# Spreading a gated recurrence over the chunks of a weight stream, on one Trainium2 core

## The chip, the cores and the metric

One core of one Trainium2 chip runs the whole program. The metric is the device time of one execution in microseconds (us). Before the change it is 1965.23 us, the median of 3 runs (1964.89 to 1965.62). The core has a matrix engine (TensorE, PE in the profile; PEld is its weight load), VectorE (DVE), ScalarE (ACT), GpSimd (POOL) and SyncE (SP, which here starts the transfers of weights). Each engine runs its own instructions strictly in their order and waits for the others by semaphores. PSUM is the memory into which PE accumulates; SBUF holds everything else.

## What is computed

One layer of a decoder for a prompt of 256 tokens and 8 samples of 8 tokens, 320 columns T in all, that share every weight. Cut to what matters here:

```python
h = rmsnorm(x) * (1 + sc1) + sh1                 # sc, sh, g: silu(c) @ w_ada
q, k, v, og, u, ga, gb, alr = split(h @ w_in)
loga = log_sigmoid(alr @ w_a2 + b_a) / 16
o, s_new = gla(q, k, v, loga, s0)                # per head: S = decay * S + k'v, o = q S
y_a = rmsnorm(o) * silu(og)
y_b = (windowed_mean(u) - u) @ w_pool * pool_scale
merged = sigmoid(ga) * y_a + sigmoid(gb) * y_b
x = x + g1 * (merged @ w_o)
x = x + g2 * swiglu(rmsnorm(x) * (1 + sc2) + sh2)   # w_gu, w_down
```

There are 4 heads; the kernel calls what belongs to one head a group (0 to 3): its 256 columns of q, k and u, and its 512 of v, og, ga and gb.

## The kernel before

Weights come as chunks of 512 KB (`raw`, 3 buffers, SP's queue). ACT rounds each to `whi` (L159, a CAST of 128x512, two to a chunk), DVE takes the rest to `wlo` (L160), and PE forms every product as three matmuls (`mm3`, L198 to L200: whi with the high part of the activations, whi with the low part, wlo with the high part), each 128 rows by 320 columns. One whi and wlo feed 12 such matmuls. `proj` makes one unit, 256 output columns: 16 row blocks, 96 matmuls, into a PSUM tile `ps`. The main PSUM pool (`pmain`) has two tiles: a unit can't begin until the unit two before it has been evacuated. A second pool of four (`pmisc`, tiles `pm`) serves everything small.

The program has a head (conditioning, h, and all projections of group 0), then the mix stage, then w_o, w_gu and w_down. The mix stage projects groups 1 to 3, unit by unit (q, k, v twice, u, og twice, ga twice, gb twice; gb of groups 1 and 3 was made in the head, `EARLY_GB`), and beside this runs the recurrence of the group before. Its steps stand in a list, `queue`, and `pump(n)` takes n of them, all at once, after each unit: `RATE` is 10, so that a lump of ten steps stands between two units. `ada_step` puts blocks of 24 more matmuls (L250, a product with w_ada; the profile shows each as two) between the chunks, in step with the stream.

The steps that matter below: `s_gk` makes the log decay from gk (on ACT: Abs L774, Exp L776, Ln L778, each with a table load of its own, ACT_TABLE_LOAD, and then two casts, L782; DVE's part of the split is L783). `s_exp(0)` and `s_exp(1)` sum it up by matmuls (L795 and L796) and take exponentials on ACT (L800 to L805). `s_prod` multiplies these with q and k (DVE, L811 to L831). `s_vstack` casts v in eight pieces (ACT, L841). `s_norm` is the normalisation of o (a matmul L1000, Sqrt L1002 on ACT, reciprocal L1003 and four products L1005 on DVE). `merge_step` multiplies with the gates (L1098) and adds (L1099). `s_y` of the pooling is the product with w_pool (tiles `psy`), evacuated by L1090.

`evac` brings a unit out of PSUM: q and k on ACT (L385), into the one buffer `g.q` that the recurrence of the group before has read until then. So the evacuation of q of group h+1 waits for the readers of q of group h, which wait for the exponentials. Group 0's gates og, ga and gb lie raw in SBUF after the head; `sig0`, the first thing in the queue, takes their sigmoids (L397, six of 128x640) and those of the early gb (L1117), with a table load wherever they stand beside another function. After the mix, ACT and DVE split the merged rows into `mh` and `ml` (L335, L336), the input of w_o; `mh12` to `mh15` are group 3's, which end last. The rows of x come back from memory by 16 transfers on SP's queue (`x<-xspill`, L1150).

Which instruction comes where on an engine is settled by a scheduler when the program is built: it starts from the order of the code and moves ready work ahead. Some instructions are pinned (`tc.keep_in_program_order`).

Of the kernel before, what the change touches and what calls it, by code (L numbers as in the profile page):

```python
# [11 lines left out]
F32 = mybir.dt.float32  # L12
# [3 lines left out]
ALU = mybir.AluOpType  # L16
# [4 lines left out]
P = 128  # L21
# [60 lines left out]
def body(tc, A):  # L82
# [131 lines left out]

    def projs(wcols, k0, k1, xh, xl):
# [100 lines left out]
    def ada_pump():  # L316
        ada_acc[0] += ada_acc[1]
        if ada_acc[0] >= 1.0 and len(ada_done) < ada_acc[2]:
            ada_acc[0] -= 1.0
            ada_step()  # L320

    def modp(sec, kt):
        return mod[:, sec * KT + kt, 0:1]

# [3 lines left out]
    def s3(ap):  # L328
        return ap.rearrange("p (b t) -> p b t", t=LS)
# [58 lines left out]
            return  # L388
        gates(g, kind, i, src)

    def gates(g, kind, i, src):
        og, gb = g.og[:, 2 * i:2 * i + 2, :], g.gb[:, 2 * i:2 * i + 2, :]
        if kind == "gb":
            S.activation(gb, src, AF.Sigmoid)
            return
        sg = gp.tile([P, 2, T], F32, tag="sg", name=nm("sg"))
        S.activation(sg, src, AF.Sigmoid)  # L397
# [346 lines left out]
    def w4(shape, dt=F32):  # L744
        return lp.tile(shape, dt, tag="w4", bufs=4, name=nm("w4"))

    def gla_steps(g):
        h = g.h
        st = []
        E = {}  # L750

# [55 lines left out]

        def s_prod():
            EQ, EK, EX, q, k = E["EQ"], E["EK"], E["EX"], g.q, g.k
            for d in range(2):  # L810
                V.tensor_tensor(qeP[:, d, :, 0:LS], s3(EQ[:, d, TP:T]), s3(q[:, d, TP:T]), op=ALU.mult)  # L811
                kk = s3(k[:, d, TP:T])
                V.tensor_tensor(keP[:, d, :, 0:LS], s3(EK[:, d, TP:T]), kk, op=ALU.mult)
                V.tensor_copy(E["dec"][:, d], s3(EQ[:, d, TP:T])[:, :, LS - 1])
# [10 lines left out]
            V.tensor_tensor(EQ[:, :, 0:TP], EQ[:, :, 0:TP], q[:, :, 0:TP], op=ALU.mult)  # L825
            V.tensor_tensor(EK[:, :, 0:TP], EK[:, :, 0:TP], k[:, :, 0:TP], op=ALU.mult)
            kq = w4([P, 2, 2, P])
            E["kdA"], E["q2"] = kq[:, 0], kq[:, 1]
            V.tensor_tensor(EX[:, :, 0:P], EX[:, :, 0:P], k[:, :, 0:P], op=ALU.mult)
            V.tensor_tensor(EX[:, :, 144:272], EX[:, :, 144:272], k[:, :, P:TP], op=ALU.mult)  # L830
            V.tensor_tensor(E["q2"], EX[:, :, 272:400], q[:, :, P:TP], op=ALU.mult)  # L831
# [159 lines left out]
        def s_norm():  # L991
# [11 lines left out]
            V.reciprocal(rs, rs)  # L1003
            for e in range(4):
                V.scalar_tensor_tensor(o[:, e], o[:, e], GNG[:, e:e + 1], rs, op0=ALU.mult, op1=ALU.mult)  # L1005
        st += [s_load(0, 0), s_load(0, 1), s_wa2, s_gk, s_exp(0), s_exp(1), s_prod, s_vstack, s_nat2, s_nat3, s_kp(0), s_attP,
               s_inter(0), s_oback(0)]
        for d in range(2):
            st += [s_state(0, d, 0), s_state(0, d, 2), s_load(1, d)]
        st += [s_att, s_nat, s_kp(1), s_o(0), s_o(1), s_sfin(0), s_sfin(1), s_inter(1), s_oback(1)]  # L1010
        for d in range(2):
            st += [s_state(1, d, 0), s_state(1, d, 2)]
        st += [s_norm]
        return st, E

    def pool_steps(g):
# [10 lines left out]
        def s_hist():  # L1027
# [7 lines left out]
        st.append(s_hist)  # L1035

        def s_buf():
            _, us = u_parts(g)
# [13 lines left out]
        st.append(s_buf)  # L1052

        def s_win():
            cur = u
# [23 lines left out]
        st.append(s_win)  # L1079

        def s_y():
            pp = [pmain.tile([P, 2, 512], F32, tag="pm", name=nm("psy")) for _ in range(2)]
            for k, whi, wlo in split_chunk(A["w_pool"][0, h].rearrange("(k p) n -> p k n", p=P), 2, 512):
                for e in range(4):
                    mm3(pp[e // 2][:, e % 2, :T], whi[:, e * P:(e + 1) * P], wlo[:, e * P:(e + 1) * P],
                        E["dh"][:, k], E["dl"][:, k], k == 0, k == 1)
            for i, ps in enumerate(pp):
# [11 lines left out]
                V.tensor_tensor(g.gb[:, e], o, g.gb[:, e], op=ALU.add)  # L1099
        return f  # L1100

    queue = []

    def pump(n):
        for _ in range(min(n, len(queue))):
            queue.pop(0)()

    tc.keep_in_program_order(nc.gpsimd.dma_start(A["o_ps"][0, :, 0:PB - LS, :], A["state_pool"][0, :, LS:PB, :]))

    st, E = gla_steps(g0)  # L1110
    pst, psy = pool_steps(g0)
    def sig0():
        for kind in ("og", "ga", "gb"):
            for i in range(2):
                gates(g0, kind, i, getattr(g0, kind)[:, 2 * i:2 * i + 2, :])
        for h in EARLY_GB:
            S.activation(merged[h], merged[h], AF.Sigmoid)  # L1117
    queue += [sig0] + pst + st[:PSY] + psy + st[PSY:] + [merge_step(g0, E)]
    RATE = 10
    ada_rate(1.0, 36)  # L1120
    for h in range(1, H):
        pump(RATE)
        g = new_group(h)
        for ui, (kind, i, col) in enumerate(units(h)):
            if kind == "gb" and h in EARLY_GB:
                continue
            if kind == "og" and i == 0:
                pump(len(queue))
# [8 lines left out]
            pump(RATE)  # L1137
        queue += psy + [merge_step(g, E)]
    pump(len(queue))


# [269 lines left out]
```

## Time and profile before

| | us |
|---|---|
| median of 3 runs | 1965.23 |
| the profiled execution | 1963.95 |
| its span, first to last instruction | 1962.2 |
| PE busy in it | 1936.7 |
| DVE busy | 1017.9 |
| ACT busy | 826.5 |
| PE busy in 300 to 350 us | 47.68 of 50 |
| PE busy in 850 to 900 us | 47.81 of 50 |

A row of a timeline has the start in us, the duration in us, the engine, the line of the code, the operation, its output and input without buffer numbers, their shapes, and in brackets how long the engine had stood idle and what released it. Where a row stands for several instructions (x2), the duration runs from the start of the first to the end of the last. A row of the windows has a stretch, then for each engine the busy time and the number of instructions, then the granted clock of TensorE as a share of full speed, the share of the DMA engines and GB/s. Matmuls of 128x320 are shown at 0.31 us, but they overlap: what counts is from start to start.

### The profile page before, as it was taken

Reading aid. Unit: us, or ns where it says so; the run is one execution under the profiler, and the core shown is the slowest. Engines: PE = TensorE matmul, PEld = TensorE weight load, DVE = VectorE, ACT = ScalarE, POOL = GpSimd, SP = SyncE. Lnnn points to the kernel's source line nnn. Section 1 sums busy time; section 2 is a strip of 40 time slices with the busy share of each in tenths; the row PEclk is TensorE's granted clock in tenths of the full one; section 3 lists DMA queues with packets and bytes.
Section 4 is the critical chain, followed back from the end, with each engine's and each line's share of the span. In section 5 each row is a group of like instructions: output and inputs, shape, how many; then the busy total and the mean of one; then the engine's idle time right before and its main releaser. Section 6 shows DMA issues by size and latency. Waiting matters only on the chain.

```text
span 1962.2 us, 37317 instructions
## 1 busy us (share of the span) xinstructions
PE 1936.7 (99%) x15060; PEld 1850.0 (94%) x15060; DVE 1017.9 (52%) x1909; ACT 826.5 (42%) x1484; POOL 135.9 (7%) x255
## 2 busy tenths in 40 slices
PE   9999999999999999999999999999999999999997
PEld 7899998898999999889999999999999999999997
DVE  3566575575456544674574444444444444444554
ACT  4333374463345433653353333433333434344443
POOL 1012220111011101010020000000000000000000
PEclk9999999999999999999999999999999999999999
DMA  9988645766976786679656666444445444444443
GB/s 321 399 275 268 194 143 180 260 232 205 321 241 209 274 269 217 204 249 323 213 183 196 222 195 193 150 151 144 153 145 153 149 150 150 150 151 146 151 139 102
DMA packets 324607, 400.84 MB, mean 204 GB/s; under 512 B 13545, under 2 KB 264681, under 8 KB 324097
## 3 DMA queue, kind: packets, MB, share of 16 engines
q1 hardware_dynamic: 312082, 357.95, 56.7%
q0 software_dynamic: 12272, 40.25, 5.6%
q8 instruction: 118, 1.93, 0.4%
q14 instruction: 55, 0.45, 0.1%
q10 hardware_dynamic: 80, 0.26, 0.0%
HBM read 373.96 MB, written 24.67 MB: 203 GB/s over the span
## 4 chain that ended last, share of the span: by engine, by line
PE 91%; DMA 1%; DVE 1%; ACT 1%; issue 0%; SPq 0%; DVEq 0%; ACTq 0%
PE ps L198 27%; PE ps L199 27%; PE ps L200 27%; PE pm L250 4%; PE pm L963 1%; PE pm L984 1%; DMA raw<-w_ada 1%; PE pm L132 1%; PE pm L928 1%; DMA raw<-w_o 0%; PE pm L917 0%; PE pm L795 0%; DMA x<-xspill 0%; PE pm L136 0%; PE pm L796 0%
## 5 line engine op out<-in xcount | busy, mean ns | idle before, releaser
L160 DVE TENSOR_TENSOR wlo<-raw,whi 128x512 fp32r<-128x512 f32 x948 | 654.0, 694 | 771.6 <-ACT whi L159 767.8
L159 ACT CAST whi<-raw 128x512 fp32r<-128x512 f32 x948 | 584.6, 621 | 973.3 <-PE ps L199 869.6
L198 PE MATMUL ps<-hh,whi 128*128 128x320 f32 x1408 | 440.7, 313 | 3.0 <-DVE mg L387 1.0
L200 PE MATMUL ps<-hh,wlo 128*128 128x320 f32 x1408 | 438.5, 312 | 0.1
L199 PE MATMUL ps<-hl,whi 128*128 128x320 f32 x1408 | 437.4, 311 | 0.7 <-DVE hl L588 0.7
L198 PE MATMUL ps<-h2h,whi 128*128 128x320 f32 x1408 | 435.8, 310 | 0.0
L199 PE MATMUL ps<-h2l,whi 128*128 128x320 f32 x1408 | 434.9, 309 | 0.8 <-DVE h2l L1261 0.8
L200 PE MATMUL ps<-h2h,wlo 128*128 128x320 f32 x1408 | 434.8, 309 | 0.0
L198 PEld LDWEIGHTS ps<-hh,whi 128*128 128x128 f32 x1408 | 264.3, 188 | 18.8 <-issue 12.0
L199 PEld LDWEIGHTS ps<-hl,whi 128*128 128x128 f32 x1408 | 264.5, 188 | 7.1 <-issue 4.6
L200 PEld LDWEIGHTS ps<-hh,wlo 128*128 128x128 f32 x1408 | 264.4, 188 | 6.2 <-issue 4.9
L198 PEld LDWEIGHTS ps<-h2h,whi 128*128 128x128 f32 x1408 | 264.1, 188 | 2.4 <-issue 2.2
L199 PEld LDWEIGHTS ps<-h2l,whi 128*128 128x128 f32 x1408 | 264.3, 188 | 1.1 <-DVE h2l L1261 1.1
L200 PEld LDWEIGHTS ps<-h2h,wlo 128*128 128x128 f32 x1408 | 264.3, 188 | 0.0
L200 PE MATMUL ps<-ah,wlo 128*128 128x320 f32 x704 | 218.1, 310 | 0.0
L199 PE MATMUL ps<-al,whi 128*128 128x320 f32 x704 | 217.6, 309 | 0.0
L198 PE MATMUL ps<-ah,whi 128*128 128x320 f32 x704 | 217.5, 309 | 0.0
L198 PEld LDWEIGHTS ps<-ah,whi 128*128 128x128 f32 x704 | 132.2, 188 | 0.0
L200 PEld LDWEIGHTS ps<-ah,wlo 128*128 128x128 f32 x704 | 132.2, 188 | 0.0
L199 PEld LDWEIGHTS ps<-al,whi 128*128 128x128 f32 x704 | 132.2, 188 | 0.0
L250 PE MATMUL pm<-raw,scT 128*32 128x128 f32 (+1 forms) x2688 | 99.5, 290 | 1.2 <-DMA raw<-w_ada 1.2
L250 PEld LDWEIGHTS pm<-raw,scT 128*32 128x32 f32 x2688 | 71.0, 109 | 22.1 <-issue 13.4
(328 smaller groups left out, 1574.0 us busy)
## 6 DMA issues: line engine op xcount, KB each, us to landing
raw<-w_ada SPq DMA_DIRECT2D x192, 512.0 KB, 6.3
raw<-w_gu SPq DMA_DIRECT2D x176, 512.0 KB, 3.4
raw<-w_in SPq DMA_DIRECT2D x173, 512.0 KB, 3.9
raw<-w_down SPq DMA_DIRECT2D x79, 512.0 KB, 3.3
S<-state_gla POOLq DMA_DIRECT2D x16, 1024.0 KB, 8.6
o_gs<-S POOLq DMA_DIRECT2D x16, 1024.0 KB, 6.2
raw<-w_o SPq DMA_DIRECT2D x32, 512.0 KB, 5.4
raw<-w_down SPq DMA_DIRECT2D x15, 256.0 KB, 2.5
```

Of the source, the lines that this page charges most:

```text
L132: PE.transpose(out, in_, ident[:k, :k])
L159: S.copy(hi, raw)
L160: V.tensor_sub(lo, raw, hi.bitcast(F32))
L198: PE.matmul(ps, lhsT=whi, rhs=xhi, start=start, stop=False)
L199: PE.matmul(ps, lhsT=whi, rhs=xlo, start=False, stop=False)
L200: PE.matmul(ps, lhsT=wlo, rhs=xhi, start=False, stop=stop)
L250: ins = PE.matmul(ps[32 * j:32 * j + 32, 0:w], lhsT=scT[:, k, :], rhs=raws[j], start=k == 0 if start is None else start, stop=k == KT - 1 ...
L928: PE.matmul(pt, lhsT=E["kdn"][:, s, d * P:(d + 1) * P], rhs=E["vn"][:, s], start=s == 0, stop=s == 1)
L963: PE.matmul(pt[32 * j:32 * j + 32, :], lhsT=qeP[:, d, 4 * gg + j, :], rhs=E["S0", gg, d][:, j], start=False, stop=d == 1, tile_position=(0 ...
L984: PE.matmul(pt, lhsT=kpz[:, j, d * P:(d + 1) * P], rhs=E["vp"][:, gg], start=True, stop=True)
```

## The change

The steps of the recurrence are joined to 15 bundles (`together`), and they are taken from the queue by `gla_pump`, called after each chunk of four row blocks in `proj`, at a rate that spreads the queue over a number of units (5 for group 0; `SPREAD`: 8, 10 and 4 for groups 1 to 3). The lumps after units, and the emptying of the queue before og, go. The sigmoids of group 0 are no longer in front: gb and og stand after six bundles, ga two bundles later, and those of the early gb stand at the evacuation of ga of group 1; all of them, and the recurrence's pinned parts of group 0, are held in program order. In `s_prod` the readers of q come first. `s_y` makes its product in two halves, one PSUM tile after the other, where it held both tiles of the main pool at once. Two steps of the pooling are one.

```diff
-PSY = 12
+PSY = 6
+SPREAD = (8, 10, 4)
...
             ada_pump()
+            gla_pump()
...
+    def gla_pump():
+        gla_acc[0] += gla_acc[1]
+        while gla_acc[0] >= 1.0:
+            gla_acc[0] -= 1.0
+            if queue:
+                queue.pop(0)()
...
-        S.activation(sg, src, AF.Sigmoid)
+        pin(S.activation(sg, src, AF.Sigmoid))
...
+            kq = w4([P, 2, 2, P])
+            E["kdA"], E["q2"] = kq[:, 0], kq[:, 1]
             for d in range(2):
+                V.tensor_copy(E["dec"][:, d], s3(EQ[:, d, TP:T])[:, :, LS - 1])
                 V.tensor_tensor(qeP[:, d, :, 0:LS], s3(EQ[:, d, TP:T]), s3(q[:, d, TP:T]), op=ALU.mult)
+            V.tensor_tensor(EQ[:, :, 0:TP], EQ[:, :, 0:TP], q[:, :, 0:TP], op=ALU.mult)
+            V.tensor_tensor(E["q2"], EX[:, :, 272:400], q[:, :, P:TP], op=ALU.mult)
...
-        st += [s_load(0, 0), s_load(0, 1), s_wa2, s_gk, s_exp(0), s_exp(1), s_prod, s_vstack, s_nat2, s_nat3, s_kp(0), s_attP,
-               s_inter(0), s_oback(0)]
...
+        st += [together(s_load(0, 0), s_load(0, 1), s_wa2), s_gk, together(s_exp(0), s_exp(1)),
+               together(s_prod, s_vstack), together(s_nat2, s_nat3, s_kp(0)), s_attP, s_inter(0),
...
-            pp = [pmain.tile([P, 2, 512], F32, tag="pm", name=nm("psy")) for _ in range(2)]
...
+            parts = list(split_chunk(A["w_pool"][0, h].rearrange("(k p) n -> p k n", p=P), 2, 512))
+            for i in range(2):
+                ps = pmain.tile([P, 2, 512], F32, tag="pm", name=nm("psy"))
...
-    queue += [sig0] + pst + st[:PSY] + psy + st[PSY:] + [merge_step(g0, E)]
-    RATE = 10
+    queue += pst + st[:PSY] + [sig0("gb"), sig0("og")] + psy + st[PSY:PSY + 2] + [sig0("ga")]
+    queue += st[PSY + 2:] + [merge_step(g0, E)]
     ada_rate(1.0, 36)
+    gla_rate(5)
...
+            if h == 1 and kind == "ga":
+                tc.keep_in_program_order(S.activation(merged[EARLY_GB[i]], merged[EARLY_GB[i]], AF.Sigmoid))
```

Where this moves instructions is seen in the programs as built. The first place is on ACT, at the evacuation of q of group 1 (output `q_...`, input the PSUM tile of that unit). `EQK` and `EX` are the exponentials of group 0, `sg` sigmoids of its gates, `w4 <- v` the casts of `s_vstack`, `whi` the weights. Before:

```order
L800 ACT_TABLE_LOAD
L800 ACTIVATE EQK_492_3323<-pm_529_3522 128x128
L802 ACTIVATE EQK_492_3323<-pm_529_3522 128x64
L800 ACTIVATE EQK_492_3323<-pm_529_3522 128x128
L802 ACTIVATE EQK_492_3323<-pm_529_3522 128x64
L803 ACTIVATE EX_494_3325<-pm_529_3522 128x144
L805 ACTIVATE EX_494_3325<-pm_529_3522 128x64
L801 ACTIVATE EQK_492_3323<-pm_530_3523 128x128 x2
L804 ACTIVATE EX_494_3325<-pm_530_3523 128x272
L841 CAST w4_533_3561<-v_15_250 128x8x8 x8
L385 ACTIVATE q_497_3343<-ps_501_3347 128x640
```

The same place after the change (the lines of the changed kernel are 13 to 16 further on here; L407 and L410 are sigmoids of gates, L816 and L819 exponentials):

```order
L820 ACTIVATE EX_528_3523<-pm_536_3575 128x64
L160 CAST whi_573_3828<-raw_570_3810 128x512
L410 ACT_TABLE_LOAD
L410 ACTIVATE sg_575_3844<-og_17_252 128x640
L160 CAST whi_578_3852<-raw_577_3850 128x512
L816 ACT_TABLE_LOAD
L816 ACTIVATE EQK_526_3521<-pm_537_3576 128x128 x2
L819 ACTIVATE EX_528_3523<-pm_537_3576 128x272
L410 ACT_TABLE_LOAD
L410 ACTIVATE sg_576_3847<-og_17_252 128x640
L857 CAST w4_545_3648<-v_15_250 128x8x8 x8
L398 ACTIVATE q_470_3235<-ps_474_3239 128x640
```

The last three exponentials of `s_exp` have been parted from the others, two sigmoids of og with their table loads stand among them, and the evacuation of q is behind all of these. On PE the next unit, `ps_564`, takes the tile of `ps_474`. Between the matmuls of gk and the first of `ps_564` PE has, in the changed program: 44 matmuls of the stream, 3 for the exponentials, 4 of the stream, 7 for the exponentials, 24 of the stream, and a block of 24 of w_ada with the last 2 for the exponentials in it.

The second place is on DVE, from the normalisation of group 3 (`acc`) to the first split rows for w_o (`ml12`). Before:

```order
L1003 RECIPROCAL acc_1456_9121<-acc_1456_9121 128x320
L160 TENSOR_TENSOR wlo_1579_10019<-raw_1575_10000,whi_1578_10018 128x512
L1090 SCALAR_TENSOR_TENSOR mg3_114<-psy_1563_9814,vec_88,mg3_114 128x320 x2
L265 TENSOR_TENSOR mod_85<-pm_1509_9466,bada_87 128x36
L160 TENSOR_TENSOR wlo_1582_10037<-raw_1580_10034,whi_1581_10036 128x512
L1005 SCALAR_TENSOR_TENSOR EQK_1398_8831<-EQK_1398_8831,vec_88,acc_1456_9121 128x320 x4
L160 TENSOR_TENSOR wlo_1584_10053<-raw_1580_10034,whi_1583_10052 128x512
L160 TENSOR_TENSOR wlo_1591_10096<-raw_1589_10093,whi_1590_10095 128x512
L1098 TENSOR_TENSOR EQK_1398_8831<-EQK_1398_8831,og_1459_9136 128x320 x4
```

And after the change (L1019 is the reciprocal, L1021, L1122 and L1123 are the products, the gates and the sum):

```order
L1019 RECIPROCAL acc_1558_9795<-acc_1558_9795 128x320
L161 TENSOR_TENSOR wlo_1619_10278<-raw_1617_10275,whi_1618_10277 128x512
L1021 SCALAR_TENSOR_TENSOR EQK_1430_9037<-EQK_1430_9037,vec_88,acc_1558_9795 128x320 x4
L1122 TENSOR_TENSOR EQK_1430_9037<-EQK_1430_9037,og_1377_8750 128x320 x3
L161 TENSOR_TENSOR wlo_1621_10294<-raw_1617_10275,whi_1620_10293 128x512
L1122 TENSOR_TENSOR EQK_1430_9037<-EQK_1430_9037,og_1377_8750 128x320
L1123 TENSOR_TENSOR mg3_114<-EQK_1430_9037,mg3_114 128x320 x3
L161 TENSOR_TENSOR wlo_1629_10329<-raw_1627_10326,whi_1628_10328 128x512
L1123 TENSOR_TENSOR mg3_114<-EQK_1430_9037,mg3_114 128x320
L349 TENSOR_TENSOR ml12_9889<-mg3_114,mh12_9873 128x320
```

DVE's chain has lost two evacuations of `psy` and some of the weights' work, which are earlier now. The third place is PE beside that chain, from the matmul of the normalisation (L1000, L1016) on. Before, it is followed by the 12 matmuls of a half of `psy` with one transpose, 24 of w_ada, 72 of w_o on rows already split (`ps_1569`), 24 of w_ada, and then the first on `mh12`. After the change the first rows are these (`ps_1597` and `ps_1569` are units of w_o):

```order
L1016 MATMUL pm_1560_9802<-acc_1558_9795,cst_76 128x320
L199 MATMUL ps_1597_10141<-mh7_9868,whi_1606_10194 128x320
L200 MATMUL ps_1597_10141<-ml7_9884,whi_1606_10194 128x320
L201 MATMUL ps_1597_10141<-mh7_9868,wlo_1607_10195 128x320
L133 MATMUL pm_1588_10090<-identr_78,adasb_1587_10088 128x128
```

They are followed by 3 more of `ps_1597`, 24 of w_ada, 24 of `ps_1597`, and then the first on `mh12`: the 72 ready matmuls that lay here have been used up ahead of the normalisation.

On SP, three chunks of w_o and three of w_ada that stood behind the 16 transfers of x now stand ahead of them.

More of the change, by code (lines that the diff above doesn't have):

```diff
@@ L320, in ada_pump @@
             ada_step()
+    queue = []
+    gla_acc = [0.0, 0.0]
+    def gla_pump():
[4 more added lines that the diff above has]
+                queue.pop(0)()
     def modp(sec, kt):
@@ L389, in evac, with gates @@
         gates(g, kind, i, src)
-    def gates(g, kind, i, src):
+    def gates(g, kind, i, src, pin=lambda ins: None):
         og, gb = g.og[:, 2 * i:2 * i + 2, :], g.gb[:, 2 * i:2 * i + 2, :]
         if kind == "gb":
-            S.activation(gb, src, AF.Sigmoid)
+            pin(S.activation(gb, src, AF.Sigmoid))
             return
         sg = gp.tile([P, 2, T], F32, tag="sg", name=nm("sg"))
-        S.activation(sg, src, AF.Sigmoid)
+        pin(S.activation(sg, src, AF.Sigmoid))
         if kind == "og":
@@ L748, in gla_steps @@
         h = g.h
+        pin = tc.keep_in_program_order if h == 0 else lambda ins: None
         st = []
@@ L809, in s_prod @@
             EQ, EK, EX, q, k = E["EQ"], E["EK"], E["EX"], g.q, g.k
+            kq = w4([P, 2, 2, P])
+            E["kdA"], E["q2"] = kq[:, 0], kq[:, 1]
             for d in range(2):
+                V.tensor_copy(E["dec"][:, d], s3(EQ[:, d, TP:T])[:, :, LS - 1])
                 V.tensor_tensor(qeP[:, d, :, 0:LS], s3(EQ[:, d, TP:T]), s3(q[:, d, TP:T]), op=ALU.mult)
+            V.tensor_tensor(EQ[:, :, 0:TP], EQ[:, :, 0:TP], q[:, :, 0:TP], op=ALU.mult)
+            V.tensor_tensor(E["q2"], EX[:, :, 272:400], q[:, :, P:TP], op=ALU.mult)
+            for d in range(2):
                 kk = s3(k[:, d, TP:T])
                 V.tensor_tensor(keP[:, d, :, 0:LS], s3(EK[:, d, TP:T]), kk, op=ALU.mult)
-                V.tensor_copy(E["dec"][:, d], s3(EQ[:, d, TP:T])[:, :, LS - 1])
             for d in range(2):
@@ L1005, in s_norm, with together, f, states @@
                 V.scalar_tensor_tensor(o[:, e], o[:, e], GNG[:, e:e + 1], rs, op0=ALU.mult, op1=ALU.mult)
-        st += [s_load(0, 0), s_load(0, 1), s_wa2, s_gk, s_exp(0), s_exp(1), s_prod, s_vstack, s_nat2, s_nat3, s_kp(0), s_attP,
-               s_inter(0), s_oback(0)]
[L1008 to L1013, printed above, removed]
+        def together(*fs):
+            def f():
+                for x in fs:
+                    x()
+            return f
+        def states(gg, d):
+            return s_state(gg, d, 0), s_state(gg, d, 2)
+        st += [together(s_load(0, 0), s_load(0, 1), s_wa2), s_gk, together(s_exp(0), s_exp(1)),
+               together(s_prod, s_vstack), together(s_nat2, s_nat3, s_kp(0)), s_attP, s_inter(0),
+               together(s_oback(0), *states(0, 0), s_load(1, 0)), together(*states(0, 1), s_load(1, 1), s_att),
+               together(s_nat, s_kp(1)), together(s_o(0), s_o(1), s_sfin(0), s_sfin(1)), s_inter(1),
+               together(s_oback(1), *states(1, 0)), together(*states(1, 1)), s_norm]
         return st, E
@@ L1081, in s_y @@
         def s_y():
-            pp = [pmain.tile([P, 2, 512], F32, tag="pm", name=nm("psy")) for _ in range(2)]
[L1083 to L1087, printed above, removed]
+            parts = list(split_chunk(A["w_pool"][0, h].rearrange("(k p) n -> p k n", p=P), 2, 512))
+            for i in range(2):
+                ps = pmain.tile([P, 2, 512], F32, tag="pm", name=nm("psy"))
+                for k, whi, wlo in parts:
+                    for e in range(2):
+                        c = (2 * i + e) * P
+                        mm3(ps[:, e, :T], whi[:, c:c + P], wlo[:, c:c + P], E["dh"][:, k], E["dl"][:, k],
+                            k == 0, k == 1)
                 for e in range(2):
@@ L1106, in pump, with gla_rate @@
             queue.pop(0)()
+    def gla_rate(nunits):
+        gla_acc[:] = [0.0, len(queue) / (4.0 * nunits)]
     tc.keep_in_program_order(nc.gpsimd.dma_start(A["o_ps"][0, :, 0:PB - LS, :], A["state_pool"][0, :, LS:PB, :]))
@@ L1111, in body, with sig0, f @@
     pst, psy = pool_steps(g0)
-    def sig0():
-        for kind in ("og", "ga", "gb"):
+    def sig0(kind):
+        def f():
             for i in range(2):
-                gates(g0, kind, i, getattr(g0, kind)[:, 2 * i:2 * i + 2, :])
-        for h in EARLY_GB:
-            S.activation(merged[h], merged[h], AF.Sigmoid)
-    queue += [sig0] + pst + st[:PSY] + psy + st[PSY:] + [merge_step(g0, E)]
-    RATE = 10
+                gates(g0, kind, i, getattr(g0, kind)[:, 2 * i:2 * i + 2, :], tc.keep_in_program_order)
+        return f
+    queue += pst + st[:PSY] + [sig0("gb"), sig0("og")] + psy + st[PSY:PSY + 2] + [sig0("ga")]
+    queue += st[PSY + 2:] + [merge_step(g0, E)]
     ada_rate(1.0, 36)
+    gla_rate(5)
     for h in range(1, H):
-        pump(RATE)
         g = new_group(h)
-        for ui, (kind, i, col) in enumerate(units(h)):
+        for kind, i, col in units(h):
             if kind == "gb" and h in EARLY_GB:
```

12 lines of the change are left out of this document (3 added, 9 removed).

## The prediction, made before the changed kernel ran

> **What bounds the kernel.** The page's list of engines comes first, then PE's waits summed over the span.
>
> ```profile
> PE 1936.7 (99%) x15060; PEld 1850.0 (94%) x15060; DVE 1017.9 (52%) x1909; ACT 826.5 (42%) x1484; POOL 135.9 (7%) x255
> L159 ACT CAST whi<-raw 128x512 fp32r<-128x512 f32 x948 | 584.6, 621 | 973.3 <-PE ps L199 869.6
> ```
> ```profile
> PE psy L198 <- ACT q L385: 2.3, 1, 2.3
> ...
> PE pm L796 <- DVE w L783: 1.4, 1, 1.4
> PE pm L250 <- DMA raw<-w_ada: 1.2, 2, 0.7
> ...
> PE pm L795 <- ACT w L782: 0.8, 1, 0.8
> PE ps L198 <- ACT mh L335: 0.7, 1, 0.7
> ```
>
> PE works 99% of the span, and the number of its matmuls stays the same. The change can therefore take away only PE's pauses (the five waits above are those at or near the mix stage, 6.4 us in all), and add others. ACT and DVE have room on average; what counts is whether a chain on them, at one place, outlasts the matmuls that PE has ready there.
>
> A pause has a second price. The timeline of PE around the longest one, and windows before and after it:
>
> ```profile
> 303.65 1.52 PE L250 MATMUL pm<-raw,scT 128*32 128x128 f32 x48
> 305.10 0.39 PE L795 MATMUL pm<-cumr,w 128*128 128x272 f32 x1
> ...
> 306.39 0.31 PE L198 MATMUL psy<-dh,whi 128*128 128x320 f32 x1
> ...
> 310.63 0.42 PE L198 MATMUL psy<-dh,whi 128*128 128x320 f32 x1 [2.32 <-ACT q L385]
> ```
> ```profile
> 255.00:300.00 45.00, 43.62 (x286) 41.65 (x285) 28.95 (x46) 34.60 (x56) 8.63 (x14) 1.00 0.47 138
> ...
> 311.00:312.00 1.00, 1.00 (x7) 1.00 (x6) 1.00 (x6) 0.20 (x1) 0.00 (x0) 0.71 0.25 94
> 312.00:313.00 1.00, 1.00 (x5) 1.00 (x5) 1.00 (x5) 0.43 (x1) 0.00 (x0) 0.50 0.00 0
> 313.00:314.00 1.00, 1.00 (x7) 1.00 (x6) 0.62 (x2) 0.61 (x1) 0.00 (x0) 0.50 0.00 0
> 314.00:315.00 1.00, 1.00 (x7) 1.00 (x6) 1.00 (x3) 0.01 (x1) 0.00 (x0) 0.59 0.51 76
> ```
>
> After the pause of 2.32 us the granted clock (the third column from the right) falls to 0.50: 0.29 + 0.50 + 0.50 + 0.41 = 1.7 us of full-speed work lost. The pause of 1.4 us (L796), at 268 us, is followed by none of that: the clock of 255 to 300 us is 1.00.
>
> **Group 0: what goes.** The pauses of 1.4 and 2.3 us and the half clock, 1.7: 5.4 us in all. The longest comes about because `psy` needed a PSUM tile that the evacuation of q had not freed; with the product in halves, and q's readers first, that wait as such is gone.
>
> **Group 0: what comes.** Now `ps_564`, the first v unit of group 1, needs that tile, and the evacuation of q stands on ACT behind `s_gk`, all exponentials, four sigmoids and the casts of v, with seven table loads from gk to q. Since ACT runs in order, the sum of these is the time from gk to q. The rows that price it, from ACT's timeline:
>
> ```profile
> 254.56 1.28 ACT L397 ACT_TABLE_LOAD   x1
> 255.86 0.74 ACT L397 ACTIVATE sg<-og 128x640 f32<-128x640 f32 x1
> ...
> 258.29 0.85 ACT L774 ACTIVATE w<-pm 128x512 f32<-128x512 f32 x2
> ...
> 261.08 0.94 ACT L776 ACTIVATE w<-w 128x512 f32<-128x512 f32 x2
> ...
> 263.84 1.12 ACT L778 ACTIVATE w<-w,onet 128x512 f32<-128x512 f32 x2
> ...
> 267.94 0.92 ACT L782 CAST w<-w 128x512 fp32r<-128x512 f32 x2
> ...
> 281.20 0.28 ACT L800 ACTIVATE EQK<-pm 128x128 f32<-128x128 f32 x1
> ...
> 282.01 1.18 ACT L159 CAST whi<-raw 128x512 fp32r<-128x512 f32 x2
> ```
> ```profile
> 306.02 0.28 ACT L800 ACTIVATE EQK<-pm 128x128 f32<-128x128 f32 x1 [0.48 <-PE pm L796]
> ...
> 307.42 1.33 ACT L841 CAST w<-v 128x64 fp32r<-128x64 f32 x8
> 309.87 0.70 ACT L385 ACTIVATE q<-ps 128x640 f32<-128x640 f32 x1 [1.11 <-DVE w L831]
> ```
>
> - `s_gk`: 0.85, 0.94, 1.12 and the casts 0.92 make 3.83; two table loads between, 2.56.
> - Six casts of weights stand among these and what follows, 6 x 0.62 = 3.7.
> - Sigmoids: two of ga and two of og, 4 x 0.74 = 3.0.
> - Exponentials: nine took 307.42 - 306.02 = 1.40, six 282.01 - 281.20 = 0.81; three more are the difference of these, 0.6. Together 2.8.
> - Five more table loads (ga; exponentials; og; exponentials; og), 5 x 1.28 = 6.4.
> - v's casts 1.33 and q itself 0.70: 2.0.
>
> Sum: 3.8 + 2.6 + 3.7 + 3.0 + 2.8 + 6.4 + 2.0 = 24.3 us, of which overlaps take a few tenths and semaphores give as much. DVE's readers of q need no more: they took 309.87 - 307.42 = 2.45 us after the last exponential, and a table load, a sigmoid and v's casts (3.3) lie beside them now.
>
> What PE has in this time, as the order of the program gives it: 72 matmuls of the stream, 12 for the exponentials, 24 of w_ada. From start to start a matmul of the stream takes, by the first and the last of a run of 24,
>
> ```profile
> 299.75 0.31 PE L199 MATMUL ps<-hl,whi 128*128 128x320 f32 x1
> ...
> 303.27 0.31 PE L199 MATMUL ps<-hl,whi 128*128 128x320 f32 x1
> ```
>
> 3.52 / 24 = 0.147 us. So 72 x 0.147 = 10.6; six for the exponentials took 306.39 - 305.10 = 1.29, twelve 2.6; the block of w_ada took 305.10 - 303.65 = 1.45. Sum 14.6. PE stands idle for 24.3 - 14.6 = 9.7 us, most of it in one piece ahead of `ps_564`. Half clock after it is taken as in the row, 1.7 (0 if the clock holds, 3.4 if it stays low twice as long). Net for group 0: 9.7 + 1.7 - 5.4 = **+6.0 us**, from 3 (a pause of 7, no half clock) to 8.
>
> [...]
>
> **Groups 1 to 3.** The 0.8 us at L795 go: 4 matmuls of the stream more (0.6 us) stand between gk and its exponentials of group 1, and the recurrence's ACT work lies thinner. For group 3 no matmuls more stand there, and I put 0.3 for a short wait like it. The evacuations of q of groups 2 and 3 aren't behind sigmoids, so nothing there. Net **-0.5**; from -0.8 to +0.8, the wait that L795 has.
>
> **The end of the mix.** The chain from the normalisation of group 3 to `mh12`, from the timelines:
>
> ```profile
> 860.01 0.70 PE L1000 MATMUL pm<-acc,cst 128*128 128x320 f32 x2
> ```
> ```profile
> 860.75 0.53 ACT L1002 ACTIVATE acc<-pm,epst 128x320 f32<-128x320 f32 x1
> ...
> 876.43 1.18 ACT L335 CAST mh<-mg 128x320 fp32r<-128x320 f32 x3
> ```
> ```profile
> 863.55 2.14 DVE L1003 RECIPROCAL acc<-acc 128x320 f32<-128x320 f32 x1
> 865.61 0.62 DVE L160 TENSOR_TENSOR wlo<-raw,whi 128x512 fp32r<-128x512 f32 x1
> ...
> 867.76 1.94 DVE L1005 SCALAR_TENSOR_TENSOR EQK<-EQK,vec,acc 128x320 f32<-128x320 f32 x4
> ...
> 870.82 1.70 DVE L1098 TENSOR_TENSOR EQK<-EQK,og 128x320 f32<-128x320 f32 x4
> ...
> 873.03 1.70 DVE L1099 TENSOR_TENSOR mg<-EQK,mg 128x320 f32<-128x320 f32 x4
> ...
> 877.25 1.29 DVE L336 TENSOR_TENSOR ml<-mg,mh 128x320 fp32r<-128x320 f32 x3
> ```
>
> From the start of the matmul to the Sqrt 860.75 - 860.01 = 0.74; Sqrt 0.53, reciprocal 2.14, two wlo 1.24, products 1.94, gates 1.70, a first sum 0.43 and a first cast 0.46 (of 1.18 for three, overlapping): 9.2 us in the changed order. PE has beside it the matmul itself (0.5, as ends overlap), 30 matmuls of w_o (4.4), a block of w_ada (1.45) and a transpose (as much as a matmul of the stream), some 6.5. Pause: 2.7 us. Before, 876.43 - 860.01 = 16.4 us lay there, with half of psy, 72 ready matmuls and two blocks of w_ada, and the wait was 0.7. Then PE does two matmuls and needs `ml12`, which DVE makes after three more sums (1.3) and a wlo (0.6) and for which it takes 0.5: 2.4 less the cast and the two matmuls, a second pause of 1.5. Half clock is likely to follow, since 2.32 us sufficed above; I put 1.0, from 0 to 1.7. Net 2.7 + 1.5 + 1.0 - 0.7 = **+4.5 us**, from 0 (all covered by work that I count as used up) to +6.
>
> [...]
>
> **Transfers.** In w_o a block of w_ada comes late, behind the rows of x on SP's queue:
>
> ```profile
> 879.62 9.33 SPq L1150 DMA_DIRECT2D x<-xspill  x16
> ```
> ```profile
> 896.85 1.52 PE L250 MATMUL pm<-raw,scT 128*32 128x128 f32 x48 [0.73 <-DMA raw<-w_ada]
> ```
>
> The queue issues nothing else for 9.33 us. Six chunks that stood behind this now stand ahead: the wait goes, **-0.7** (from -1.2, all waits on w_ada, to 0). The rest of the change (bundles, no emptying at og, two pooling steps in one) moves small matmuls among the stream, and their number stays: 0, at most 1 either way, the size of the waits in the list.
>
> **Sum.** 6.0 - 0.5 + 4.5 - 0.7 = +9.3 us. The profiled execution took 1963.95 us (its span 1962.2 and 1.75 around it, which stays), so 1973.25; the median of the runs, 1965.23, lies 1.3 above it, and by it the time is **1974.5 us**.
>
> **The rivals.**
> - *Faster*: ACT's chain is covered. It would do if q's evacuation ran within PE's 14.6 us; then the pauses of before go, and with the tail covered too that is 5.4 + 0.8 + 0.7 = 6.9 less, 1958. For it speaks ACT's 42% on average; against it the order of ACT, in which nothing can pass the sigmoids. Chance 0.07.
> - *The new wait only takes the place of the old*: the chain on ACT starts earlier than gk's end suggests or runs closer, so that group 0's pause is 5 us and not 9.7, and the tail costs half: 9.3 - 4.7 - 2.3 = +2.3, 1967.5. For it: the chain is a sum of rows from a busier stretch. Chance 0.13.
> - *Slower still*: the clock stays low for two of the stretches seen after the long pause (+1.7), is halved fully in the tail (+0.7), and the transfers give nothing (+0.7): 3.1 more, 1977.6. Chance 0.08.
> - [...] Chance 0.02. [...]
>
> **The numbers.** The forecast has 0.70, with 1969 to 1978 from its own bounds. With the third case and most of the second the range is 1966.5 to 1979. A measurement of this kernel can tell about 0.2%, 3.9 us, from no change: below 1961.3 is only the first rival, 0.07; from there to 1969.1 lies the second with a sliver of the forecast, 0.15; the rest is 0.78.
>
> **What would show it.** In the profile after: among PE's waits one of some 8 us, of a `ps` on ACT's evacuation of q (L398), between 315 and 330 us (the block of w_ada ahead of gk is now the one that ran at 303.65), and a window of half clock after it; one of about 2.8 on `mh` (L348) and one near 1.5 on `ml` (L349) after 860; none on q by `psy`. On ACT, between gk and q, seven table loads in a row of work without a gap. It would be wrong if q's evacuation came within 16 us of gk, or if PE showed other work between gk and `ps_564` than counted.

## The result and the profile after

The changed kernel took 1978.93 us, median of 4 runs (1976.7 to 1983.69), against 1965.06 before: 1.0074 times as long, 95% interval 1.0054 to 1.0094. Five more runs beside a kernel before of 1965.08 (e9 below) gave 1976.21 and a ratio of 1.0058 (1.0045 to 1.0072). So it is slower, as forecast, by 11 to 14 us where 9.3 were forecast. The profiled execution of the 4 took 1980.35, 16.4 more than that of before.

A word on what was told ahead: in the changed kernel only the sigmoids and the early gb's are held in order; the `pin` that `gla_steps` defines is used nowhere. And the sigmoids at L407, which the prediction counted as ga, are those of gb.

PE's waits of the changed kernel, the longest first (us in all, times, longest):

```profile
PE ps L199 <- ACT q L398: 7.8, 1, 7.8
PE ps L199 <- ACT mh L348: 2.5, 1, 2.5
...
PE pm L979 <- DMA S<-state_gla: 2.1, 1, 2.1
PE ps L200 <- DVE ml L349: 1.2, 1, 1.2
```

Three were forecast, at 8, 2.8 and 1.5. The wait on the state S (L979) was not, nor one on x in the head, shown below. The windows of before and of after over the same three stretches, group 0, groups 1 and 2, and the end of the mix with w_o:

```profile
255.00:350.00 95.00, 91.30 (x698) 85.19 (x697) 59.47 (x115) 56.05 (x106) 11.53 (x18) 0.98 0.54 163
350.00:820.00 470.00, 468.72 (x3956) 430.83 (x3957) 261.31 (x534) 217.08 (x419) 52.64 (x86) 1.00 0.73 243
820.00:1000.00 180.00, 176.81 (x1530) 165.74 (x1530) 104.53 (x220) 72.89 (x140) 16.65 (x32) 1.00 0.76 255
```
```profile
255.00:350.00 95.00, 86.73 (x646) 83.80 (x645) 52.60 (x106) 49.63 (x97) 6.03 (x13) 0.96 0.51 153
350.00:820.00 470.00, 469.00 (x3974) 430.48 (x3973) 260.54 (x520) 220.69 (x412) 59.91 (x91) 1.00 0.74 243
820.00:1000.00 180.00, 173.56 (x1452) 160.72 (x1451) 104.97 (x227) 74.86 (x146) 14.15 (x24) 0.98 0.73 243
```

PE's idle time is the stretch less its busy time: 3.7 us before and 8.3 after in the first, 1.3 and 1.0 in the second, 3.2 and 6.4 in the third. In the first and the third the clock has fallen further, too, from 0.98 to 0.96 and from 1.00 to 0.98 (the third column from the right). Where the long pause lies, on ACT and on PE of the changed kernel:

```profile
308.65 0.95 ACT L789 ACTIVATE w<-pm 128x512 f32<-128x512 f32 x2 [0.59 <-PE pm L779]
...
324.17 1.28 ACT L410 ACT_TABLE_LOAD   x1
325.46 0.74 ACT L410 ACTIVATE sg<-og 128x640 f32<-128x640 f32 x1
...
331.86 0.69 ACT L398 ACTIVATE q<-ps 128x640 f32<-128x640 f32 x1
```
```profile
332.61 0.63 PE L199 MATMUL ps<-hh,whi 128*128 128x320 f32 x1 [7.83 <-ACT q L398]
```

From gk to the end of q's evacuation ACT took 332.55 - 308.65 = 23.9 us without a gap (24.3 forecast). PE's work beside it lasted to 332.61 - 7.83 = 324.78. At the end of the mix, on PE, the two products with the last states of group 3, and a block of w_ada in w_o:

```profile
868.53 1.06 PE L979 MATMUL pm<-S,qeP 128*32 128x512 f32 x8
875.36 1.22 PE L979 MATMUL pm<-S,qeP 128*32 128x512 f32 x8 [2.06 <-DMA S<-state_gla]
...
931.92 1.08 PE L252 MATMUL pm<-raw,scT 128*32 128x128 f32 x32 [0.70 <-DMA raw<-w_ada]
```

And in the head, where the programs of both kernels are the same on PE, the dummy matmuls that keep PE busy until x comes, before and after:

```profile
8.78 3.37 PE L441 MATMUL idle<-fill 128*128 128x512 f32 x9
```
```profile
7.44 2.32 PE L454 MATMUL idle<-fill 128*128 128x512 f32 x9
10.83 0.55 PE L458 MATMUL pm<-identr,xn 128*128 128x128 f32 x3 [1.07 <-DMA xn<-x_prompt]
```

Nine of them took 3.37 us in one execution and 2.32 in the other, so in the second they ran out before x was there. Later in the head, from 16 to 26 us, the clock stood at 0.50, and the first product on h began at 35.54 us, not at 31.72. From 36 to 40 us the clock was low once more (0.73, 0.50, 0.50 and 0.56, another 1.7 us), where the execution before had 1.00. So 3.8 and 1.7 of the 16.4 us lie ahead of everything that the change moved, and 10.9 are left. That the wait for x brought the half clock of the head is not shown; e10 below speaks against it.

### The profile page after: what moved, and what is told of

Read it like the earlier page. It is cut to its first block, busy times and chain, and to the rows that moved or that the text cites. A ratio compares the mean times of both kernels' runs of the same rounds, so it can differ in the third digit from the quotient of the medians.

```text
span 1978.6 us, 37326 instructions
## 1 busy us (share of the span) xinstructions
PE 1944.2 (98%) x15060; PEld 1855.6 (94%) x15060; DVE 1016.7 (51%) x1909; ACT 830.1 (42%) x1485; POOL 137.6 (7%) x255
## 4 chain that ended last, share of the span: by engine, by line
PE 89%; DMA 2%; ACT 1%; DVE 1%; issue 1%; POOL 0%; DVEq 0%; ACTq 0%; POOLq 0%
PE ps L199 27%; PE ps L200 26%; PE ps L201 26%; PE pm L252 4%; PE pm L1000 1%; PE pm L979 1%; PE pm L133 1%; DMA raw<-w_in 1%; PE pm L944 1%; DMA o_gs<-S 0%; DMA raw<-w_ada 0%; DMA S<-state_gla 0%; PE pm L933 0%; ACT whi L160 0%; PE pm L137 0%
## 5 line engine op out<-in xcount | busy, mean ns | idle before, releaser
L252 PE MATMUL pm<-raw,scT 128*32 128x128 f32 (+1 forms) x2688 | 103.5, 293 | 1.1 <-DMA raw<-w_ada 1.1
```

The source lines that it names most:

```text
L252: ins = PE.matmul(ps[32 * j:32 * j + 32, 0:w], lhsT=scT[:, k, :], rhs=raws[j], start=k == 0 if start is None else start, stop=k == KT - 1 ...
```

## The experiments

**e1. The sigmoids not held in order.**

```diff
-                gates(g0, kind, i, getattr(g0, kind)[:, 2 * i:2 * i + 2, :], tc.keep_in_program_order)
+                gates(g0, kind, i, getattr(g0, kind)[:, 2 * i:2 * i + 2, :])
```

> The changed kernel with one thing undone: the sigmoids of group 0 are no longer held in program order, so that the program as built has them ahead of gk again and only three table loads between gk and the evacuation of q, not seven. Theory A (the wait ahead of the first v unit is the length of ACT's chain): the chain from gk to q loses 2.55 us of sigmoids and four loads of 1.29, 7.7 us; the wait of 7.83 us on q (L398) falls below 0.5, the wait of 0.44 at the exponentials goes, and the half clock that follows goes with them (2.1 us). About 10 us less than the changed kernel: 1965 to 1969. Rival B (q's evacuation is late because of its readers on DVE, or because of PSUM, whatever stands on ACT): the wait stays above 5 us and the time within 3 us of the changed kernel's 1976.5 to 1980.

Measured: 1968.69 us (1964.37 to 1971.03, 11 runs), 1.0016 times before (1.0007 to 1.0025), 7.5 to 10 less than the changed kernel's two medians. ACT from gk to q, and PE's waits:

```profile
304.65 0.95 ACT L789 ACTIVATE w<-pm 128x512 f32<-128x512 f32 x2 [0.58 <-PE pm L779]
...
313.38 1.28 ACT L815 ACT_TABLE_LOAD   x1
...
320.84 0.70 ACT L398 ACTIVATE q<-ps 128x640 f32<-128x640 f32 x1
```
```profile
PE ps L199 <- ACT mh L348: 2.5, 1, 2.5
...
PE ps L199 <- ACT q L398: 1.3, 1, 1.3
```

With three table loads, the one of the row and two in `s_gk`, the way from gk to q's end is 321.54 - 304.65 = 16.9 us, 7.0 shorter, and the wait on q falls from 7.8 to 1.3 (below 0.5 was expected). ACT's chain set the pause. At the end of the mix the waits stay: 2.5 us on mh, and on the state 1.6 where it was 2.1.

**e2. Both stores of the state ahead of both loads, in group 3.** The stores and loads of that group are held in order as well:

```diff
-together(s_oback(0), *states(0, 0), s_load(1, 0)), together(*states(0, 1), s_load(1, 1), s_att),
+together(s_oback(0), *states(0, 0)), together(*states(0, 1), s_load(1, 0), s_load(1, 1), s_att),
```

> The changed kernel with group 3's two stores of the state issued before the next two loads on GpSimd's queue, as it was before the change, in place of store, load, store, load. Theory A (the wait of 2.06 us on the state at the second product with it comes from GpSimd standing at a load until the first store has landed, which holds back the second store and so the second load): the second load goes out about 862 instead of 868.6, lands before PE needs it, and the wait goes, with the half clock after it (1.7 us). 3.5 to 4 us less than the changed kernel; the waits on mh and ml stay. Rival B (the state's transfers are slow because they share the DMA engines with the weights): the wait stays at 1.5 us or more and the time doesn't move by over 1 us.

Measured: 1976.28 us (1972.98 to 1980.87, 5 runs), ratio 1.0058 (1.0045 to 1.0072). GpSimd's queue before the change, in the changed kernel and in e2, and PE in e2:

```profile
822.62 0.82 POOL L988 DMA_DIRECT2D o_gs<-S  x1 [25.69 <-DVE S L986]
...
833.27 0.76 POOL L951 DMA_DIRECT2D S<-state_gla  x1 [3.75 <-DMA o_gs<-S]
```
```profile
846.99 0.84 POOL L1004 DMA_DIRECT2D o_gs<-S  x1 [6.49 <-DVE S L1002]
855.88 0.77 POOL L967 DMA_DIRECT2D S<-state_gla  x1 [8.05 <-DMA o_gs<-S]
856.64 0.75 POOL L1004 DMA_DIRECT2D o_gs<-S  x1
...
868.64 0.79 POOL L967 DMA_DIRECT2D S<-state_gla  x1 [9.54 <-DMA o_gs<-S]
```
```profile
843.05 0.79 POOL L1006 DMA_DIRECT2D o_gs<-S  x1 [6.48 <-DVE S L1004]
849.51 0.76 POOL L1006 DMA_DIRECT2D o_gs<-S  x1 [5.67 <-DVE S L1004]
851.85 0.75 POOL L969 DMA_DIRECT2D S<-state_gla  x1 [1.57 <-DMA o_gs<-S]
...
860.79 0.79 POOL L969 DMA_DIRECT2D S<-state_gla  x1 [5.59 <-DMA o_gs<-S]
```
```profile
869.09 1.93 PE L981 MATMUL pm<-S,qeP 128*32 128x512 f32 x8 [2.21 <-DMA S<-state_gla]
```

Before the change the second load went out 833.27 - 822.62 = 10.65 us after the first store, and PE made its second product with the state at 843.77 without a wait. In the changed kernel it goes out after 868.64 - 846.99 = 21.65 us, in e2 after 860.79 - 843.05 = 17.7. Yet in e2 the wait stays, 2.2 us: the second load now takes over 8 us to land (out at 860.79, PE goes on at 869.09), and the program as built has moved the second product 18 matmuls ahead. The time is that of the changed kernel in e9 (1976.21). Theory A, that the order on the queue was the cause, is not borne out.

**e3. Group 3 over 3 units.**

```diff
-SPREAD = (8, 10, 4)
+SPREAD = (8, 10, 3)
```

> The changed kernel with the steps of group 3 spread over 3 units and not 4. In the program as built 66 matmuls of w_o and a block of w_ada now stand between the normalisation and mh12, about 11 us, for a chain of 9.2. Theory A (the end's pauses are the chain less the work that is left for PE): the waits on mh and ml, 2.5 and 1.2 us, go with their half clock of 1.6, 5.3 us less. But the steps come faster one after the other: from the first store of the state to the second product PE has some 20 us, where the transfers, one after the other, took 28.4 in the changed kernel: the wait on the state grows from 2.1 to 6 to 9 us. In all within 4 us of the changed kernel. Rival B (the wait on the state is a matter of the DMA engines' load alone): the loads just take 7 us, the wait stays near 2, and the kernel is 5 us faster than the changed one.

Measured: 1964.89 us (1963.17 to 1968.69, 11 runs), ratio 1.0002 (0.9993 to 1.0011): 11 to 14 less than the changed kernel. The long wait on q is all that is left of those above. POOL and PE of e3:

```profile
838.25 0.84 POOL L1004 DMA_DIRECT2D o_gs<-S  x1 [2.91 <-DVE S L1002]
843.78 0.77 POOL L967 DMA_DIRECT2D S<-state_gla  x1 [4.69 <-DMA o_gs<-S]
844.54 0.75 POOL L1004 DMA_DIRECT2D o_gs<-S  x1
854.10 0.75 POOL L967 DMA_DIRECT2D S<-state_gla  x1 [8.80 <-DMA o_gs<-S]
```
```profile
859.83 1.07 PE L979 MATMUL pm<-S,qeP 128*32 128x512 f32 x8
861.46 1.07 PE L979 MATMUL pm<-S,qeP 128*32 128x512 f32 x8
```

The waits on mh and ml are gone, as the chain's length against PE's work said. But the wait on the state, which theory A had at 6 to 9 us, is gone too. The order is still store, load, store, load; only the transfers are quicker: 15.85 us from the first store to the second load where it was 21.65. So the run came out far below the range of 4 us about the changed kernel that was expected. PE came to the first product 859.83 - 838.25 = 21.6 us after the first store, as in the changed kernel (868.53 - 846.99 = 21.5). So it is not PE's pace or the order that made the wait, but how long the way from store to load takes at that moment. The windows of 22 us from the first store, in the changed kernel and in e3, end with the share of the DMA engines and GB/s:

```profile
847.00:869.00 22.00, 22.00 (x208) 17.19 (x210) 14.14 (x29) 9.30 (x18) 4.26 (x5) 1.00 0.93 327
```
```profile
838.00:860.00 22.00, 22.00 (x160) 18.71 (x162) 14.07 (x29) 11.43 (x23) 5.25 (x6) 1.00 0.87 299
```

The engines are fuller in the changed kernel (0.93 against 0.87), where more of the chunks of w_o and w_ada fall into this stretch. That this is the reason is argued from these two rows; no run changed the traffic of the weights alone.

**e7. No stores of the first two states of group 3.** That part of the output is left out.

```diff
-                if j0 == 2:
+                if j0 == 2 and not (h == H - 1 and gg == 0):
```

> The changed kernel without the stores of the first two states of group 3 (that part of the output o_gs is left out): the loads into the same buffers then wait only for DVE's last use, and 2 MB fewer are moved there. Theory A (the wait on the state at its second product is the way from store to load, whichever queue order it has and however loaded the DMA engines are): the loads go out about 847 and 852, land before 865, and the wait of 2.1 us and its half clock of 1.7 go: 3 to 4 us less than the changed kernel, 1972 to 1975; the waits on mh and ml stay. Rival B (the load alone takes too long, since the weights fill the DMA engines): the wait stays above 1 us.

Measured: 1968.8 us (1966.97 to 1972.16, 11 runs), ratio 1.0015 (1.0006 to 1.0023), 7 to 10 less than the changed kernel. POOL and PE:

```profile
842.67 0.84 POOL L967 DMA_DIRECT2D S<-state_gla  x1 [6.49 <-DVE S L1002]
849.12 0.77 POOL L967 DMA_DIRECT2D S<-state_gla  x1 [5.62 <-DVE S L1002]
```
```profile
864.39 1.92 PE L979 MATMUL pm<-S,qeP 128*32 128x512 f32 x16
```

Without the store to wait for, both loads are out 6.5 us apart, and PE makes all products with the state in one go. It gave more than the 3 to 4 us expected, since the waits on mh and ml went too: the program as built has the matmul of the normalisation 23 matmuls earlier, and what lay ahead of it now lies beside the chain. So the end's pauses hang together, here by the order in which the program is built. The edit takes away two things, the store that a load must wait for and 2 MB of traffic (the share of the DMA engines from 842 to 864 us is 0.80), and this run doesn't part them.

**e4 and e8. The edits together.** e4 is e1, e2 and e3 at once; e8 is e1 and e3 without e2.

> All three edits together: no sigmoids held in order, both stores ahead of both loads in group 3, steps of group 3 over 3 units. Theory A: group 0 gives 10 us, the end 5.3, and the wait on the state is 0 to 3 us, since from the first store to the second load's landing some 22 us are needed and PE has 20; so 1976.7 - 10 - 5.3 - 3.8 + 0 to 4.7, 1958 to 1963, faster than the kernel before by 2 to 7 us. Rival B (the bundles themselves cost, by PE's many short matmuls among the stream): not below 1965.

> The version with all three edits, but without the order of stores and loads on GpSimd's queue: no sigmoids held in order, and group 3 over 3 units. Theory A (in that place the order is of no account, as the waits in the run with 3 units alone show none on the state): within 1 us of the version with all three, 1955 to 1958. Rival B (the order was worth its 2.6 us there as it was in the run by itself): 1958.5 to 1960.

Measured: e4 1956.27 us (1955.3 to 1957.43, 5 runs), ratio 0.9956 (0.9944 to 0.9969). e8 1956.37 us (1954.96 to 1961.55, 6 runs), ratio 0.9953 (0.9938 to 0.9967). Two lines of edit make the changed kernel 9 us faster than the kernel before, and the order on GpSimd's queue is worth nothing here. e4 came out below the 1958 to 1963 that was expected. The two gains add up: e1 and e3 lie 7.5 and 11.3 us below the changed kernel's median in e9, 18.8 together, and e8 lies 19.8 below it. e8's windows:

```profile
255.00:350.00 95.00, 93.31 (x727) 87.92 (x726) 53.75 (x106) 49.87 (x102) 9.24 (x15) 1.00 0.55 171
350.00:820.00 470.00, 470.00 (x3973) 433.30 (x3972) 265.86 (x541) 222.34 (x425) 56.19 (x89) 1.00 0.74 244
820.00:1000.00 180.00, 178.62 (x1544) 167.77 (x1543) 111.77 (x244) 78.26 (x154) 23.10 (x46) 1.00 0.75 252
```

PE idles 1.7, 0.0 and 1.4 us there, where the kernel before had 3.7, 1.3 and 3.2, and the clock is 1.00 in all three. So the change leaves PE fewer pauses once two of its settings are altered; these two, the pins of the sigmoids and the spread of group 3, were what cost. That the rest of the gain comes from the bundles beside each chunk is argued: no run has the bundles alone, and e5 and e6 below only show that two other parts give nothing by themselves.

**e5 and e6. Two parts of the change on the kernel before**: the product with w_pool in halves (e5), and with it q's readers first (e6). The edits are those of the diff for `s_y` and `s_prod`, alone.

> The kernel before with one part of the change alone: the product with w_pool in two halves, one PSUM tile after the other. In the program as built PE's order is that of before, and the second half still takes the tile from which q is evacuated. Theory A (what PE waits for there is q's evacuation, and that waits for its readers): the wait of 2.3 us of psy on q (L385) stays as it is, with the half clock, and the time is that of before, within 1 us. Rival B (the two tiles held at once are the cause, as the prediction had it in part): the wait goes, 2.3 and 1.7 us less.

> The kernel before with two parts of the change: the halves, and q's readers first on DVE. Theory A: the last reader of q ends about 308.6 instead of 309.8 us, q's evacuation then waits only for the casts of v (308.75), and PE goes on about 309.5 instead of 310.6: a wait of 1.2 us on q, as the 1.3 that e1 and e4 still show, too short for half clock (1.4 and 1.6 us were, in before and in e1): 1.1 + 1.7 less, 2 to 3.5 us faster than before. Rival B (the readers' order doesn't matter, the gain of the version with all three edits is that of the bundles alone): within 1 us of before.

Measured: e5 1965.54 us (12 runs), ratio 0.9998 (0.9989 to 1.0007); e6 1965.15 us (11 runs), ratio 0.9999 (0.9990 to 1.0008). The wait of psy on q is 2.3 us in e5, as before the change; in e6:

```profile
PE psy L198 <- ACT q L385: 1.9, 1, 1.9
```

The halves change nothing there, as theory A had it; q's readers first save 0.4 us and not the 1.1 expected, and the half clock still follows (0.98 from 255 to 350 us, as before; from 312.54 on a matmul of the stream takes 0.27 us from start to start), and the time is that of before, where 2 to 3.5 us less were expected. So these two parts, by themselves, don't take away that wait; in the versions with all of the change it falls to 1.3, with the bundles in another place.

**e9 and e10. More runs of the changed kernel, and more dummy matmuls in its head.**

```diff
-            keep_busy((9, 6, 0)[i])
+            keep_busy((14, 6, 0)[i])
```

> The changed kernel as it is, for a scatter of more runs than four. Theory A (its profile holds 3.8 us that have nothing to do with the change: TensorE's clock came up early, the dummy matmuls of the head ran out 1.07 us before the rows of x came, and the clock then fell): the runs without that lie at 1975 to 1978, and single ones 2 to 5 us above; the median is 1977 +- 1.5. Rival B (the change itself slows the head): the median stays at 1979 or above and the profile again shows the first product at 35 us or later.

> The changed kernel with 14 dummy matmuls in place of 9 ahead of the second block of x. Theory A: where the clock comes up early the five more (1.3 us at 0.26) bridge the wait of 1.07 for x, so that the head's loss of 4 us no longer occurs; where it comes up late they cost up to 1.9 (0.37 each) in the head. The runs lie closer together, none above 1981, median within 2 us of the changed kernel's. Rival B (the scatter comes from the half clock after the pauses in the mix, not from the head): the same scatter as the changed kernel beside it.

Measured: e9 1976.21 us (1974.55 to 1979.55, 5 runs), ratio 1.0058 (1.0045 to 1.0072); its first product on h begins at 32.48 us, so the 35.54 of the first profile is not the change's. e10 1977.47 us (1973.53 to 1978.81, 5 runs), ratio 1.0058 (1.0045 to 1.0070). In e10's profile the dummies were quick again, 14 of them in 3.47 us where e9's nine took 4.14, and PE didn't wait for x behind them:

```profile
7.20 3.47 PE L454 MATMUL idle<-fill 128*128 128x512 f32 x14
```

So the wait for x is bridged, as theory A has it. But the clock fell in the head all the same, for 3.4 us from 15 us on (0.63, 0.50, 0.50 and 0.66 in the four windows to 19 us):

```profile
16.00:17.00 1.00, 1.00 (x24) 0.76 (x13) 0.61 (x4) 0.31 (x2) 0.00 (x0) 0.50 1.11 350
```

The first product on h begins at 32.48 us, just as in e9 with nine dummies. In e6 PE waited for x twice, 0.71 and 1.78 us; the six dummies behind the second took 1.64 us, as in the kernel before, and from 31 to 40.5 us the clock was 1.00. What the clock of e6 was between 14 and 28 us is not shown. In e10 it fell with no more than 0.28 us of waiting for x ahead of it, so that wait is not needed for it, and what halves the clock there stays open. The runs lie as far apart as those of e9, so how much of the scatter comes from the head stays open too.

## Why the prediction was wrong

Its direction and its main mechanism were right: ACT's chain from gk to q in group 0 outlasts PE's work (shown by e1), and the chain from the normalisation to mh outlasts what is left of w_o (shown by e3). The size was too small, by 2 us against e9 and 4.6 against the first median; by the first ratio the time is 1965.23 x 1.0074 = 1979.8, above the upper end of the range, 1979; by the ratio of e9 it is 1965.23 x 1.0058 = 1976.6, within it. Which side it falls on is thus partly chance, but one step failed either way. Step by step, from the profiles, with the windows of the changed kernel after the pause on q and after the one on the state:

```profile
332.61:337.00 4.39, 4.39 (x17) 4.39 (x18) 0.94 (x5) 1.15 (x2) 0.00 (x0) 0.52 0.00 2
876.00:880.00 4.00, 4.00 (x18) 3.49 (x15) 0.69 (x1) 1.20 (x2) 0.56 (x1) 0.57 0.84 313
```

- **Group 0: 6.0 forecast, about 5 measured.** ACT's chain was 23.9 for 24.3. PE's work was mis-sized: 14.6 forecast; measured 324.78 - 308.65 = 16.1, less the idle time of the stretch beside the long pause, 8.27 - 7.83 = 0.44: 15.7 (0.5 more are matmuls of gk that still ran when ACT had begun, 0.5 the block of w_ada, which ran in two parts). The pauses are 8.3 us, not 9.7. (The lower bound of 3 doesn't follow from its own terms: a pause of 7 and no half clock give 7 - 5.4 = 1.6.) The clock was already low when PE went on, and from there it cost 4.39 x 0.48 = 2.1. What went was 5.4, as counted: 8.3 + 2.1 - 5.4 = 5.0. The reason given for what went (halves and q's readers) is not borne out by e5 and e6, so why these 5.4 went is not shown.
- **Groups 1 to 3: -0.5 forecast, -0.3 measured** (1.3 to 1.0 us idle).
- **The end of the mix: this step failed.** The pauses on mh and ml were right (2.7 and 1.5 forecast, 2.5 and 1.2 measured; the 1.5 should have been 1.6 by its own terms), and the half clock after them was 1.7 for 1.0. But the step followed the chain only from the normalisation on. Ahead of it lies another, state stored, next state loaded into the same buffer, product with it, on GpSimd's queue; the prediction looked at SP's queue alone. PE came to that product 2.06 us too early, and half clock followed, 4 x 0.43 = 1.7. These two are 3.8 us that stand in no term of the sum; the rest of the change, the bundles of steps among it, had been put at 0, at most 1 either way. In e9's profile of the same kernel the wait on the state was 1.55 us with no half clock after it, and the half clock after mh and ml 3.4 for 1.7: so the missing term is 1.6 to 3.8 us. Why the way from store to load took 21.65 us and not 10.65 as before stays open; that the DMA engines were fuller is argued in e3.
- **Transfers: the wait goes, -0.7. Not in this profile:** a block of w_ada is late by 0.70 at 931.92, where one was by 0.73 at 896.85 before. In e9's profile none is late there.
- **The head: 0 forecast.** 3.8 us in the profiled execution, and 1.7 of half clock behind the first product on h, none of it by the change; the first median holds an unknown share.

Of the rivals it was the third, slower still. Its terms came in this profile: 2.1 for 1.7 after the long pause, 1.7 for 1.0 in the tail, nothing from the transfers, 1.8 us more in all. But its main part was the state's wait, which it did not name. The switch of table sets cost its load alone, as the rows of before said: 324.17 + 1.28 = 325.45, and the sigmoid starts at 325.46.

## What to carry to other kernels

Work that is spread evenly over a stream is not yet in the right order on the other engines: follow one in-order engine from the first to the last instruction of the chain that a PSUM tile waits for, count every table load on it, and set the sum against the matmuls that the stream has there. At the end of a stage do the same for every chain that the last step needs, transfers through other queues and buffers that must first be stored among them. And judge such a change only with its settings varied: here one number and one flag lay between 11 us lost and 9 gained.

## What the runs showed of the hardware

The length of a pause alone doesn't decide whether the clock is halved. In the mix it looks as if it did: in the kernel before 2.3 us did it (0.50 after it) and 1.4 didn't (1.00 from 255 to 300 us); 1.6 us on the state, in e1 and in e9, didn't (1.00 from 847 to 869 us and from 865 to 890 us), 1.9 in e6 did (0.98 from 255 to 350 us). But the pause of 1.00 us ahead of the first product on h, the same in every profile, was followed by half clock in 7 of the 12 profiles (0.76 from 31 to 38 us, 0.73 and less from 36 to 40 in the changed kernel's first) and not in 5 (1.00). e1 and e4, whose programs on PE are the same up to there, from 31 to 38 us:

```profile
31.00:38.00 7.00, 6.23 (x25) 5.36 (x26) 4.83 (x9) 3.97 (x9) 1.30 (x3) 0.76 0.85 256
```
```profile
31.00:38.00 7.00, 6.23 (x36) 5.35 (x36) 4.82 (x9) 4.71 (x10) 1.31 (x3) 1.00 0.86 250
```

What was lost in the head and the mix, where windows of 1 us show it, came in portions of 1.7 us, 3.4 us of half clock each: one after the pause on the state, two around the end of the 7.8 us in the changed kernel (from 330 to 336.8 us), three in its head (from 16 to 26.2 us, 5.1 in all). In e3, which has no such windows, the mean of 0.95 from 255 to 350 us makes 95 x 0.05 = 4.8 us, about three. What of a portion lies within a pause costs nothing: in the changed kernel PE stood idle in the first 2.6 of the 6.8 us, and the rest cost 4.39 x 0.48 = 2.1. Why the same pause is followed by half clock in one execution and not in another is not shown.
